# A final norm on VectorE alone, five weight buffers, and other queues for rows and form sources in a Strassen-form MLP

## The chip, the core and the metric

The kernel runs on one core of a Trainium2 chip. A core has five engines with instruction streams of their own: TensorE (PE in the profile, PEld for its weight loads), VectorE (DVE), ScalarE (ACT), GpSimd (POOL) and SyncE (SP). ACT, POOL and SP can each issue DMA transfers, in the order of their own streams. The metric is the device time of one execution in microseconds, as a median of several runs.

## The reference, cut to what matters

One layer of an encoder, in float32, on two batches with the same weights: `x_prompt` (512 tokens) and `x_sample` (1024 tokens), 1024 features each.

```
h = rms_norm(x, g_mix);  proj = h @ w_in                 # q, k, v, z, gates
merged = sigmoid(ga) * (attention @ w_branch_a) + sigmoid(gb) * (spatial gating @ w_branch_b)
x = x + merged @ w_out
h2 = rms_norm(x, g_mlp)
x = x + square(relu(h2 @ w_up)) @ w_down                 # w_up 1024 x 4096, w_down 4096 x 1024
y = rms_norm(x, g_final)
```

The change concerns the last three lines.

## The kernel before

**Products.** Every matrix product is made of float32r matmuls. A float32 operand is split into `hi` (a cast on ACT, L150) and `lo` (source minus hi, a subtraction on DVE, L151), and a product takes three matmuls (hi*hi, hi*lo, lo*hi). `weight` (L153 on) brings a weight block of 128 x 512: SP loads it into a buffer `raw` (L156, a ring of `N_RAW` = 3), ACT casts it and DVE subtracts, into a ring of five hi/lo pairs.

**Before the MLP.** Norm, projections, attention, gating and w_out run until about 1752 us. The last loop (L748 on) goes over the twelve token tiles t of 128 tokens: it adds `merged @ w_out` to x, stores the sum to `x1_scr` on SP's queue (L776), scales it by its root mean square (L782), transposes the halves on PE (L741), multiplies by `g_mlp` on DVE into `h2T` (L743, a ring of two buffers) and stores that to `h2_scr` on SP's queue (L746). The transposes of a tile come after the first matmuls of the next, so those of tile 11 come last of all.

**The MLP.** It takes the 1536 tokens as two groups g of 768 (tiles 0 to 5 and 6 to 11) and the 4096 hidden features as eight chunks c. Each product of a chunk is done by a form of Strassen's method with seven products, called p1, q6, q7, p2, q5, q4, q3, in place of eight. The sums of weight blocks that it needs were made during attention and lie in DRAM (`up_q`, `down_q`); those of activations are made on DVE. A chunk has two calls of `up_products` (j = 0, 1; together "an up stage": 2 x 7 forms of 12 matmuls of 128x384) and one of `down_products` (a "down stage": 126 matmuls of 128x512).

In an up stage each form's PSUM result is combined at once: p1 is copied by ACT (L888), then DVE makes v, z and the four blocks a11, a22, a21, a12 (L891 to L911), ACT applies relu and square (L870, L871), and `Forms.put`, `sums` and `last` build and split the seven forms of the activation (`act`; L817 to L819 and L828 on DVE, casts and subtractions in L150 and L151). In a down stage the results are added into rows `x` on DVE (L942 to L958) and, for a part, on POOL (L949, L950, L960).

Small tiles of 128x384 (`unit`, L797) come from one ring of twelve: p1, v, z, a, s, the form sources `h`, the differences `diff` and `raw_form`.

**Order.** Nothing sets times by hand but a list of side steps: `side()` is called after each form of an up stage and after each tile of a down stage, and runs the next step of the list. Engines run their own streams in order, and a DMA issue that waits for a buffer holds up what stands behind it in its queue.

- At the start of the MLP (L1062 to L1072), for each of four k: SP loads four form sources `h` from `h2_scr` (L1067), and ACT and DVE make the seven forms `hf` from them.
- `load_rows` (L1049) loads the group's six tiles of x, 512 KB each, from `x1_scr` on POOL's queue (L1052). It is called after c = 0's up stage; for g = 0 nothing holds the loads back but their buffers.
- For group 1 the sums of h are made in side steps of chunks 1 to 4 (`diff_steps`, loads and stores on SP's queue), and its `hf` forms in side steps of chunk 7 (`form_steps`, loads at L1013 on SP's queue).
- The final norm of group 0 runs as side steps in group 1's first up stage (`final_steps` with `spread`): squares on ACT, the root on DVE, then for each of twelve half tiles a scaling on ACT (L1038), a multiplication by g_final on POOL (L1039) and a store on POOL's queue (L1040). The rows of group 1 then take the same buffers.
- The final norm of group 1 comes at the end, as one DVE operation for each half tile (`normed`, L234).

Of the kernel before, what the change touches and what calls it, by code (L numbers as in the profile page):

```python
# [10 lines left out]
F32 = mybir.dt.float32  # L11
# [21 lines left out]
BIG = 1e30  # L33
ROW = 2 * 64 + 4
EDGE = 24
N_SPLIT, N_RAW = 5, 3
QT = 2
STEPS = 49 / 36
XSTEP = 4
# [67 lines left out]
def encoder_kernel(ctx: ExitStack, tc: tile.TileContext, a):  # L107
# [24 lines left out]
    v_scr = dram.tile([NTOK, NG * 512], F32, name="v_scr")  # L132
    gate_scr = [dram.tile([P, NTOK], F32, name=f"gate_scr{m}") for m in range(EARLY)]
    form_scr = dram.tile([len(DIFFS), 4, P, HT], F32, name="form_scr")
    h2_scr = dram.tile([KB, P, NTOK], F32, name="h2_scr")
    x1_scr = dram.tile([NTOK, DM], F32, name="x1_scr")
    up_sums = {k: dram.tile([DM // 2, DFF // 2], F32, name=f"up_{k}") for k in SUMS}
    down_sums = {k: dram.tile([DFF // 2, DM // 2], F32, name=f"down_{k}") for k in SUMS}
# [10 lines left out]
    def split(hi, lo, src, eng=nc.vector):  # L149
        nc.scalar.copy(hi, src)  # L150
        eng.tensor_sub(lo, src, hi.bitcast(F32))  # L151

    def weight(src, k, pair=None, eng=nc.vector):  # L153

        raw = wp.tile([P, 512], F32, tag="raw", name="raw", bufs=N_RAW).rearrange("p (k n) -> p k n", k=k)
        nc.sync.dma_start(out=raw, in_=src.rearrange("(k p) n -> p k n", p=P))  # L156
        if pair is None:
            pair = (wp.tile([P, 512], F32R, tag=s, name=s, bufs=N_SPLIT) for s in ("hi", "lo"))
        hi, lo = (t.rearrange("p (k n) -> p k n", k=k) for t in pair)
        split(hi, lo, raw, eng)  # L160
        return hi, lo
# [574 lines left out]
    def h_features(t, halves):  # L736

        for i, h in enumerate(halves):
            pt = tp_tile()
            for b in range(4):  # L740
                nc.tensor.transpose(pt[:, b * P:(b + 1) * P], h[:, b * P:(b + 1) * P], ident)  # L741
            hT2 = pp.tile([P, 512], F32, tag="half", name="h2T", bufs=2)
            nc.vector.tensor_mul(  # L743
                hT2.rearrange("p (k t) -> p k t", k=4), pt.rearrange("p (k t) -> p k t", k=4),
                g_mlp[:, 4 * i:4 * i + 4, None].to_broadcast([P, 4, P]))
            nc.sync.dma_start(  # L746
                out=h2_scr[4 * i:4 * i + 4, :, t * P:(t + 1) * P].rearrange("k p t -> p k t"),
                in_=hT2.rearrange("p (k t) -> p k t", k=4))  # L748

    for ch in range(2):  # L750
# [45 lines left out]
    slabs = ctx.enter_context(tc.tile_pool(name="slabs", bufs=6, side="right", reuse_waits="tile"))  # L796
    ps3 = ctx.enter_context(tc.tile_pool(name="ps3", bufs=8, space=PSUM, reuse_waits="tile"))  # L797
    def unit(name):
        return mp.tile([P, HT], F32, tag="unit", name=name, bufs=12)

    def bank():
        return ps3.tile([P, 512], F32, tag="acc", name="acc")
# [47 lines left out]
            self(len(self.steps))  # L850

    side = Side()

    def slab_view(s):
        return s.rearrange("p a b c -> p (a b c)").bitcast(F32)[:, :DM]
# [8 lines left out]
    def up_products(hf, j, forms, between):  # L864

        c = slice(j * P, (j + 1) * P)
        held = {}

        def squared(x, src):
            nc.scalar.activation(x, src, AF.Relu)  # L870
            nc.scalar.activation(x, x, AF.Square)  # L871

        for form in UP_ORDER:
            w = weight(block_of(a["w_up"][0], up_sums, form, DM // 2, DFF // 2, slice(0, DM // 2), c), 4)
            on = {"p2": "p1", "q3": "q5"}.get(form)
            acc = held[on] if on else bank()
            held[form] = acc
            acc = acc[:, :HT]
            for k in range(4):
                sh, sl = (x[:, k, :] for x in w)  # L880
                mh, ml = hf[k].of(form)
                for n, (st, mv) in enumerate(((sh, mh), (sh, ml), (sl, mh))):
                    nc.tensor.matmul(  # L883
                        acc, st, mv, start=not on and k == 0 and n == 0, stop=k == 3 and n == 2,
                        skip_group_check=bool(on))
            if form == "p1":
                p1 = unit("p1")
                nc.scalar.copy(p1, acc)  # L888
            elif form == "q6":
                v = unit("v")  # L890
                nc.vector.tensor_sub(v, acc, p1)  # L891
            elif form == "p2":
                a11 = unit("a11")
                squared(a11, acc)
                forms.put("p1", a11)
            elif form == "q7":
                z = unit("z")
                nc.vector.tensor_sub(z, v, acc)
            elif form == "q5":
                a22 = unit("a22")  # L900
                nc.vector.tensor_add(a22, z, acc)
                squared(a22, a22)
                forms.put("q4", a22)
            elif form == "q4":
                a21 = unit("a21")
                nc.vector.tensor_sub(a21, acc, z)
                squared(a21, a21)
                s2 = forms.sums(a11, a21, a22)
            elif form == "q3":
                a12 = unit("a12")  # L910
                nc.vector.tensor_add(a12, v, acc)  # L911
                squared(a12, a12)
                forms.last(a12, s2)
            between(form)
# [50 lines left out]
    def diff_steps(k):  # L965

        x = {}

        def load(key, r, s):
            x[key] = unit("diff")  # L970
            nc.sync.dma_start(out=x[key], in_=h2_scr[4 * s + k, :, GT + r * HT:GT + (r + 1) * HT])

        def store(form, key):
            nc.sync.dma_start(out=form_scr[DIFFS.index(form), k], in_=x[key])

        def first():
            load("a", 0, 0)
            load("b", 1, 0)
            nc.vector.tensor_sub(x["a"], x["a"], x["b"])
            store("q7", "a")  # L980

        def second():
            load("c", 1, 1)
            nc.vector.tensor_sub(x["b"], x["b"], x["c"])
            store("q5", "b")

        def third():
            nc.vector.tensor_add(x["c"], x["a"], x["c"])
            store("q6", "c")

        def fourth():
            load("d", 0, 1)
            nc.vector.tensor_sub(x["d"], x["d"], x["c"])
            store("q3", "d")

        return [first, second, third, fourth]

    def form_source(form, k):
        if form in DIFFS:
            return form_scr[DIFFS.index(form), k]  # L1000
        r, s = {"p1": (0, 0), "p2": (0, 1), "q4": (1, 1)}[form]
        return h2_scr[4 * s + k, :, GT + r * HT:GT + (r + 1) * HT]

    def form_steps(fs):

# [13 lines left out]
    def final_steps(g, x, tiles, g_final, spread):  # L1019
# [12 lines left out]
        def rows(j, i):  # L1032
# [2 lines left out]
            y = y_rows[6 * g + tiles[j]][:, i * 512:(i + 1) * 512]  # L1035
            gf = g_final[i]
            if spread:
                nc.scalar.activation(r, r, AF.Copy, scale=scale)  # L1038
                nc.gpsimd.tensor_mul(r, r, gf)  # L1039
                nc.gpsimd.dma_start(out=y, in_=r)  # L1040
            else:
                normed(r, r, scale, gf)
                (nc.scalar, nc.sync)[i].dma_start(out=y, in_=r)
# [4 lines left out]
    def load_rows(g):  # L1048
        x = {}  # L1049
        for t in (3, 4, 5, 0, 1, 2):  # L1050
            x[t] = mp.tile([P, DM], F32, tag="x", name="x", bufs=6)
            nc.gpsimd.dma_start(out=x[t], in_=x1_scr[(6 * g + t) * P:(6 * g + t + 1) * P, :])  # L1052
        return x

    def gains():
# [2 lines left out]
            load_g(g_final[i], a["g_final"][i * 512:(i + 1) * 512])  # L1058
        return g_final


    hf = {k: Forms("hf") for k in (3, 0, 1, 2)}  # L1062
    for k in range(4):
        parts = {}
        for s, r in ((0, 0), (0, 1), (1, 1), (1, 0)):
            parts[r, s] = unit(f"h{r}{s}")
            nc.sync.dma_start(out=parts[r, s], in_=h2_scr[4 * s + k, :, r * HT:(r + 1) * HT])  # L1067
        hf[k].put("p1", parts[0, 0])
        s2 = hf[k].sums(parts[0, 0], parts[1, 0], parts[1, 1])
        hf[k].put("q4", parts[1, 1])  # L1070
# [58 lines left out]
```

## Time and profile before

| | |
|---|---|
| median of 3 runs | 2783.99 us (2783.96 to 2785.03) |
| the profiled execution's own time | 2783.46 us |
| its span in the trace | 2781.7 us |
| mean granted TensorE clock | 0.987 |
| first up stage of group 0, from PE's first matmul | 1771.31 us |
| first down stage of group 0 | 1815.62 us |
| up and down stage of chunk 7, group 0 | 2198.44 and 2228.55 us |
| up stage of chunk 0, group 1 | 2266.46 us |
| its down stage | 2325.81 us |
| last down stage | 2734.63 us |

A row of the timeline has the start, the time that it spans, the engine, the line, the operation, output<-input, the shape and the count; in brackets the idle time of the engine before it and what ended that. "SPq" is an issue of a DMA. In the rows of waits stand the engine and tile that waited, what it waited for, the sum, the number and the longest. Names are those of the program without numbers; `h_scr` is `h2_scr`, `x_scr` is `x1_scr`, `s` are the sums s1 to s4, `p` is p1 in an up stage, `z` and `v` likewise.

### The profile page before, as it was taken

The page shows a single profiled execution, that of the slowest core. Times are in us where ns is not written, and L with a number is a line of the kernel's source. Part 1 is how long each engine was busy: PE and PEld are TensorE (multiplying, and loading weights), DVE is VectorE, ACT ScalarE, POOL GpSimd, SP SyncE. Part 2 cuts the span into 40 slices and gives each one's busy share as a digit, 9 for nine tenths or more (in the row PEclk, how much of TensorE's full clock was granted, in tenths as well). Part 3 has the DMA queues.
Part 4 walks back from the last instruction along what each step waited for, and adds up shares of the span by engine and source line. Part 5 has one row for each costly group of instructions (what it writes and reads, how often), then busy time and mean ns, then how long its engine had stood idle before and what let it go on. Part 6 is the DMA issues. An engine that isn't in the chain of part 4 may idle for free.

```text
span 2781.7 us, 38699 instructions
## 1 busy us (share of the span) xinstructions
PE 2681.2 (96%) x13400; PEld 2297.2 (83%) x13400; DVE 1731.4 (62%) x3665; ACT 1296.4 (47%) x2778; POOL 392.3 (14%) x418
## 2 busy tenths in 40 slices
PE   7999999999999999999999999699999978999997
PEld 5788888888888887888888888588889967998896
DVE  6542200166666666555555436688888887888887
ACT  5321111255566556553534321455555564665555
POOL 2000000011021212100000000022322134111321
PEclk9999999999999999999999999899999998999999
DMA  3112222237576767554444435545454455444443
GB/s 132 51 52 72 89 76 80 87 109 177 156 171 184 169 180 177 143 157 147 128 147 119 126 136 170 165 135 160 152 151 129 140 164 179 125 132 125 125 128 128
DMA packets 374516, 373.57 MB, mean 134 GB/s; under 512 B 21936, under 2 KB 294832, under 8 KB 370736
## 3 DMA queue, kind: packets, MB, share of 16 engines
q1 hardware_dynamic: 343344, 262.51, 31.4%
q0 software_dynamic: 21584, 66.90, 10.4%
q10 hardware_dynamic: 9392, 41.69, 4.5%
q8 instruction: 106, 1.74, 0.3%
q14 instruction: 90, 0.74, 0.1%
HBM read 321.95 MB, written 116.16 MB: 158 GB/s over the span
## 4 chain that ended last, share of the span: by engine, by line
PE 37%; DVE 8%; issue 5%; ACT 4%; DMA 3%; POOL 2%; SPq 0%; DVEq 0%; ACTq 0%; POOLq 0%
PE acc L933 9%; PE acc L175 7%; PE acc L176 7%; PE acc L177 7%; PE acc L883 6%; DVE lo L151 3%; DMA raw<-up_q 1%; ACT hi L150 1%; POOL x L950 1%; POOL x L949 1%; DVE act L151 1%; ACT a L870 1%; ACT a L871 1%; ACT act L150 1%; DVE x L958 1%
## 5 line engine op out<-in xcount | busy, mean ns | idle before, releaser
L151 DVE TENSOR_TENSOR lo<-raw,hi 128x512 fp32r<-128x512 f32 x694 | 545.1, 791 | 406.3 <-ACT hi L150 400.2
L150 ACT CAST hi<-raw 128x512 fp32r<-128x512 f32 x696 | 430.6, 620 | 647.0 <-PE acc L176 230.3
L175 PE MATMUL acc<-res_h,hi 128*128 128x512 f32 x1344 | 556.5, 414 | 0.8 <-DVE stg L576 0.8
L177 PE MATMUL acc<-res_h,lo 128*128 128x512 f32 x1344 | 526.8, 392 | 0.0
L176 PE MATMUL acc<-res_l,hi 128*128 128x512 f32 x1344 | 525.5, 391 | 0.0
L883 PE MATMUL acc<-hf,hi 128*128 128x384 f32 x1792 | 468.2, 342 | 42.0 <-ACT hf L150 16.8
L933 PE MATMUL acc<-hi,act 128*128 128x512 f32 x1344 | 420.2, 392 | 1.6 <-ACT hi L150 1.6
L883 PEld LDWEIGHTS acc<-hf,hi 128*128 128x128 f32 x1792 | 327.8, 191 | 56.7 <-ACT hf L150 20.6
L883 PE MATMUL acc<-hf,lo 128*128 128x384 f32 x896 | 303.4, 339 | 3.7 <-DVE lo L151 3.6
L933 PEld LDWEIGHTS acc<-hi,act 128*128 128x128 f32 x1344 | 254.3, 189 | 54.5 <-ACT hi L150 2.0
L177 PEld LDWEIGHTS acc<-res_h,lo 128*128 128x128 f32 x1344 | 252.6, 188 | 54.9
L175 PEld LDWEIGHTS acc<-res_h,hi 128*128 128x128 f32 x1344 | 254.1, 189 | 36.6 <-DVE stg L576 0.9
L176 PEld LDWEIGHTS acc<-res_l,hi 128*128 128x128 f32 x1344 | 254.5, 189 | 36.0
L933 PE MATMUL acc<-lo,act 128*128 128x512 f32 x672 | 264.7, 394 | 7.3 <-DVE lo L151 7.3
L548 ACT ACTIVATE pr<-pr,stg 128x128 f32<-128x128 f32 (+2 forms) x288 | 125.9, 438 | 177.1 <-DVE stg L545 140.7
L883 PEld LDWEIGHTS acc<-hf,lo 128*128 128x128 f32 x896 | 171.0, 191 | 5.2 <-DVE lo L151 5.2
L949 POOL TENSOR_TENSOR x<-x,z 128x512 f32<-128x512 f32 x48 | 71.2, 1484 | 623.0 <-DVE z L948 623.0
L933 PEld LDWEIGHTS acc<-lo,act 128*128 128x128 f32 x672 | 127.2, 189 | 37.0 <-DVE lo L151 10.7
L518 DVE TENSOR_TENSOR q<-qT,q 64x256 fp32r<-64x256 f32 x288 | 120.6, 419 | 48.0 <-ACT q L515 44.3
L560 DVE COPY pT<-tp 128x512 f32<-128x512 f32 (+1 forms) x144 | 82.1, 570 | 94.7 <-PE tp L558 93.7
L570 PEld LDWEIGHTS o<-v,pT 128*128 128x128 f32 x896 | 120.3, 191 | 25.0 <-DVE pT L560 14.7
L570 PE MATMUL o<-v,pT 128*128 128x64 f32 x896 | 117.3, 268 | 7.9 <-DVE pT L560 7.7
(183 smaller groups left out, 4081.8 us busy)
## 6 DMA issues: line engine op xcount, KB each, us to landing
raw<-in_w_in_dram SPq DMA_DIRECT2D x192, 256.0 KB, 3.1
raw<-up_q SPq DMA_DIRECT2D x128, 256.0 KB, 2.8
raw<-down_q SPq DMA_DIRECT2D x128, 256.0 KB, 2.7
raw<-in_w_up_dram SPq DMA_DIRECT2D x96, 256.0 KB, 2.8
raw<-in_w_down_dram SPq DMA_DIRECT2D x96, 256.0 KB, 2.8
up_q<-in_w_up_dram POOLq DMA_DIRECT2D x32, 512.0 KB, 9.2
down_q<-in_w_down_dram POOLq DMA_DIRECT2D x32, 512.0 KB, 10.4
raw<-in_w_branch_b_dram SPq DMA_DIRECT2D x48, 256.0 KB, 2.9
```

Source lines behind the costliest of these rows:

```text
L150: nc.scalar.copy(hi, src)
L151: eng.tensor_sub(lo, src, hi.bitcast(F32))
L175: nc.tensor.matmul(out, sh, mh, start=i == 0, stop=False)
L176: nc.tensor.matmul(out, sh, ml, start=False, stop=False)
L177: nc.tensor.matmul(out, sl, mh, start=False, stop=i == n - 1)
L518: nc.vector.tensor_sub(q2[rows, h, 1, :], src, q2[own, h, 0, :].bitcast(F32))
L548: last_of["act"] = nc.scalar.activation(pr[:, h, at:at + kn], pr[:, h, at:at + kn], AF.Exp, bias=low, scale=-1.0, accum_out=stg[:, j, 130 ...
L560: nc.vector.tensor_copy(self.pT[:, :n], pt[:, :n])
L570: nc.tensor.matmul(o[:, (2 * j + h) * 64:(2 * j + h + 1) * 64], self.pT[:, q * P:(q + 1) * P], found["v"][:, slot, h * 64:(h + 1) * 64], s ...
L883: nc.tensor.matmul(acc, st, mv, start=not on and k == 0 and n == 0, stop=k == 3 and n == 2, skip_group_check=bool(on))
L933: nc.tensor.matmul(acc, st, mv, start=not on and k == 0 and n == 0, stop=k == 1 and n == 2, skip_group_check=bool(on))
L949: nc.gpsimd.tensor_sub(x21, x21, z)
```

## The change

The norm of group 0 (`spread`) becomes one `normed` on DVE for each half tile; the stores stay on POOL's queue. In the MLP the raw ring grows from three to five buffers (two of them in the MLP's pool), and the ring of units shrinks from twelve to ten. `h2_scr` becomes one DRAM tensor for each group. The sixteen form sources of group 0 are loaded on POOL's queue instead of SP's, and the four `hf` slabs are taken in the order 0, 1, 2, 3. The rows of x for group 0 are loaded on ACT's queue instead of POOL's, and the loads for both groups may be issued only after the last p1 copy of chunk 0's up stage. All else, up to the MLP and at the program's end, is as it was.

```diff
-N_SPLIT, N_RAW = 5, 3
+N_SPLIT, N_RAW, MORE_RAW = 5, 3, 2
...
-    h2_scr = dram.tile([KB, P, NTOK], F32, name="h2_scr")
+    h2_scr = [dram.tile([KB, P, GT], F32, name=f"h2_scr{g}") for g in range(2)]
...
+    more_raw = []
+    def raw_tile():
+        pool, bufs = wp, N_RAW
+        if more_raw:
+            at = more_raw[1] = (more_raw[1] + 1) % (N_RAW + MORE_RAW)
+            if at >= N_RAW:
+                pool, bufs = more_raw[0], MORE_RAW
+        return pool.tile([P, 512], F32, tag="raw", name="raw", bufs=bufs)
...
     def unit(name):
-        return mp.tile([P, HT], F32, tag="unit", name=name, bufs=12)
+        return mp.tile([P, HT], F32, tag="unit", name=name, bufs=10)
...
     side = Side()
+    more_raw += [mp, 0]
...
             if form == "p1":
                 p1 = unit("p1")
-                nc.scalar.copy(p1, acc)
+                last_of["up"] = nc.scalar.copy(p1, acc)
...
             if spread:
-                nc.scalar.activation(r, r, AF.Copy, scale=scale)
-                nc.gpsimd.tensor_mul(r, r, gf)
+                normed(r, r, scale, gf)
                 nc.gpsimd.dma_start(out=y, in_=r)
...
         for t in (3, 4, 5, 0, 1, 2):
             x[t] = mp.tile([P, DM], F32, tag="x", name="x", bufs=6)
-            nc.gpsimd.dma_start(out=x[t], in_=x1_scr[(6 * g + t) * P:(6 * g + t + 1) * P, :])
+            eng = nc.gpsimd
+            if not g:
+                eng = nc.scalar
+            with tc.issue_after(last_of["up"].ins):
+                eng.dma_start(out=x[t], in_=x1_scr[(6 * g + t) * P:(6 * g + t + 1) * P, :])
...
-    hf = {k: Forms("hf") for k in (3, 0, 1, 2)}
+    hf = {k: Forms("hf") for k in range(4)}
     for k in range(4):
...
             parts[r, s] = unit(f"h{r}{s}")
-            nc.sync.dma_start(out=parts[r, s], in_=h2_scr[4 * s + k, :, r * HT:(r + 1) * HT])
+            nc.gpsimd.dma_start(out=parts[r, s], in_=h2_scr[0][4 * s + k, :, r * HT:(r + 1) * HT])
```

The rows of an engine's order below carry the line numbers of the changed kernel where they show it: from `weight` on its lines stand 11 higher, after `side` by 12 (L888 is L900, L911 is L923), L1040 is L1051, L1052 is L1067 and L1067 is L1081.

More of the change, by code (lines that the diff above doesn't have):

```diff
@@ L151, in split @@
         eng.tensor_sub(lo, src, hi.bitcast(F32))
+    more_raw = []
[6 more added lines that the diff above has]
+        return pool.tile([P, 512], F32, tag="raw", name="raw", bufs=bufs)
     def weight(src, k, pair=None, eng=nc.vector):
-        raw = wp.tile([P, 512], F32, tag="raw", name="raw", bufs=N_RAW).rearrange("p (k n) -> p k n", k=k)
+        raw = raw_tile().rearrange("p (k n) -> p k n", k=k)
         nc.sync.dma_start(out=raw, in_=src.rearrange("(k p) n -> p k n", p=P))
@@ L746, in h_features @@
             nc.sync.dma_start(
-                out=h2_scr[4 * i:4 * i + 4, :, t * P:(t + 1) * P].rearrange("k p t -> p k t"),
+                out=h2_scr[t // 6][4 * i:4 * i + 4, :, t % 6 * P:(t % 6 + 1) * P].rearrange("k p t -> p k t"),
                 in_=hT2.rearrange("p (k t) -> p k t", k=4))
@@ L970, in load @@
             x[key] = unit("diff")
-            nc.sync.dma_start(out=x[key], in_=h2_scr[4 * s + k, :, GT + r * HT:GT + (r + 1) * HT])
+            nc.sync.dma_start(out=x[key], in_=h2_scr[1][4 * s + k, :, r * HT:(r + 1) * HT])
         def store(form, key):
@@ L1001, in form_source @@
         r, s = {"p1": (0, 0), "p2": (0, 1), "q4": (1, 1)}[form]
-        return h2_scr[4 * s + k, :, GT + r * HT:GT + (r + 1) * HT]
+        return h2_scr[1][4 * s + k, :, r * HT:(r + 1) * HT]
     def form_steps(fs):
```

## The prediction

> **What bounds the kernel now.** I read the page's engine shares and its slices first, then windows of busy time, then the waits and the timeline where the windows dip.
>
> ```profile
> PE 2681.2 (96%) x13400; PEld 2297.2 (83%) x13400; DVE 1731.4 (62%) x3665; ACT 1296.4 (47%) x2778; POOL 392.3 (14%) x418
> ...
> PE   7999999999999999999999999699999978999997
> ```
>
> TensorE (PE) is the limit nearly everywhere: only slices 26, 33 and 34 dip inside the program. Windows give these dips (start and end, sum, then PE, PEld, DVE, ACT and POOL busy, the granted clock, DMA share, GB/s):
>
> ```profile
> 1750.00:1800.00 50.00, 28.89 (x111) 22.12 (x110) 33.11 (x78) 18.13 (x40) 2.63 (x5) 0.73 0.57 181
> 1800.00:1850.00 50.00, 49.68 (x248) 44.38 (x247) 42.86 (x71) 28.24 (x56) 13.39 (x9) 1.00 0.42 126
> 2228.00:2266.00 38.00, 30.73 (x116) 23.00 (x115) 35.14 (x58) 22.74 (x49) 10.04 (x8) 0.91 0.60 187
> 2266.00:2290.00 24.00, 21.93 (x111) 19.11 (x111) 17.99 (x37) 18.89 (x47) 9.12 (x8) 1.00 0.41 122
> 2290.00:2310.00 20.00, 7.91 (x30) 7.40 (x31) 20.00 (x13) 9.34 (x19) 19.60 (x24) 0.66 0.65 211
> 2310.00:2326.00 16.00, 9.56 (x45) 9.27 (x44) 7.30 (x14) 7.44 (x15) 1.10 (x3) 0.74 0.79 264
> 2326.00:2355.00 29.00, 29.00 (x126) 23.89 (x125) 23.01 (x36) 12.03 (x23) 8.90 (x6) 0.97 0.36 109
> 2355.00:2385.00 30.00, 29.27 (x168) 28.83 (x167) 24.77 (x41) 20.17 (x40) 4.68 (x3) 1.00 0.47 138
> ```
>
> The last two rows are a down stage of the MLP, 126 matmuls in 29.0 us, and an ordinary up stage, 168 in about 29.5. The first row is the **boundary** where the MLP begins. Rows three to six are the **switch** from token group 0 to group 1: chunk 7's down stage (2228 to 2266) and group 1's first up stage (2266 to 2326). That up stage takes 60 us for the work of 29.5. VectorE (DVE) is busy for all 20 us from 2290, GpSimd (POOL) for 19.6, and PE for 7.9. PE's waits over the switch (total, times, longest) say for whom:
>
> ```profile
> PE acc L883 <- ACT hi L150: 10.7, 3, 10.1
> PE acc L933 <- DVE lo L151: 6.8, 4, 3.0
> PE acc L883 <- DVE a L901: 6.4, 1, 6.4
> PE acc L883 <- DVE lo L151: 3.6, 3, 3.1
> ```
>
> **The boundary.** From its timeline:
>
> ```profile
> 1757.20 1.34 PE L741 MATMUL tp<-ident,h 128*128 128x128 f32 x8 [3.50 <-DVE h L782]
> 1765.00 1.33 DVE L743 TENSOR_TENSOR h2T<-tp,g_mlp 128x512 f32<-128x512 f32 x2 [7.55 <-DMA h_scr<-h2T]
> 1770.75 0.51 ACT L150 CAST hf<-h 128x384 fp32r<-128x384 f32 x1 [16.38 <-DMA h<-h_scr]
> 1752.82 2.67 POOL L1052 DMA_DIRECT2D x<-x_scr  x5 [32.29 <-DVE h L782]
> 1767.12 16.25 SPq L1067 DMA_DIRECT2D h<-h_scr  x16
> 1782.47 0.56 DVE L151 TENSOR_TENSOR hf<-s,hf 128x384 fp32r<-128x384 f32 x1 [0.58 <-ACT hf L150]
> 1788.29 0.56 DVE L151 TENSOR_TENSOR hf<-s,hf 128x384 fp32r<-128x384 f32 x1 [0.58 <-ACT hf L150]
> ```
>
> The last transposes end at 1758.54, yet their multiply starts at 1765.00: its buffer's store is still under way, behind five x loads of 512 KB (the fourth row). Then come the form sources on SP, and the first cast at 1770.75. From there DVE sets the pace: 5.82 us for each k of the forms (the last two rows).
>
> On POOL, before:
>
> ```order
> L467 DMA o_scr_83<-stg 64x4x132 x4
> L728 DMA g_mlp<-in_g_mlp_dram 128x8x1
> L1052 DMA x<-x_scr 128x1024 x6
> L949 TENSOR_TENSOR x<-x,z 128x512
> L950 TENSOR_TENSOR x<-x,z 128x512
> ```
>
> and now:
>
> ```order
> L478 DMA o_scr_83<-stg 64x4x132 x4
> L739 DMA g_mlp<-in_g_mlp_dram 128x8x1
> L1081 DMA h_15122<-h_scr_96 128x384
> L1081 DMA h_15124<-h_scr_96 128x384
> L1081 DMA h_15126<-h_scr_96 128x384
> ```
>
> The x rows' place is taken by sixteen form sources. Their scratch half holds tiles 0 to 5, stored long before, so they no longer wait for the last stores. But the first of them lands in memory that g_mlp held, so by the built program's waits it goes out only once the last h2T multiply has run: they do not move up into w_out. Without the x loads the multiply can start at 1758.6 and end at 1759.9; the first load then issues there instead of at 1767.12, 7.2 us earlier, and the first cast with it. Two things take back part. The first cast's tile lies over h2T buffers, so it needs the last h2T stores landed too, about when the first h load lands. And three weights that DVE split earlier now stand among the first forms, at 0.69 us each, with raws that SP fetches only then. I take **-4 us**, between -7 (all of it) and -1 (the split weights' loads arrive last).
>
> In this row of SP's queue a raw lands as usual in under 3 us, and in the next POOL's 256 KB stores in 2.4:
>
> ```profile
> raw<-up_q SPq DMA_DIRECT2D x128, 256.0 KB, 2.8
> ...
> sgu_scr<-u POOLq DMA_DIRECT2D x24, 256.0 KB, 2.4
> ```
>
> So I price the change of queue at nothing. The Trainium skill ("DMA: Bandwidth & Descriptors", Latency and other measured facts) gives the GpSimd path a first byte about 0.4 us later than SP's; by that the sum would be 0.4 us higher. The rows show no such difference, though they compare a store with a load.
>
> **The x rows of group 0** now go out on ACT's queue after chunk 0's second p1 copy:
>
> ```order
> L900 COPY p_15437<-acc 128x384
> L1067 DMA x<-x_scr 128x1024 x2
> L882 ACTIVATE a_15499<-acc 128x384
> L1067 DMA x<-x_scr 128x1024
> L883 ACTIVATE a_15499<-a_15499 128x384
> ```
>
> ACT issued no DMA here before; it now pays six issues, at POOL's 2.67/5 = 0.53 us some 3 us, in a window where it works 28.24 of 50. Their 3 MB join 126 GB/s (second window) where 264 GB/s were carried at 2310 to 2326. The rows are needed when the down stage begins, some 12 us (six forms) after that copy. A raw that is delayed is covered by five buffers at 2.1 us a form. I take **+1**, from 0 to +3.
>
> **Five raws, ten units.** In chunk 7's down stage PE takes 38 us for the 126 matmuls that take 29.0 in the next one: 9 lost, with 6.8 us of waits on lo. More raws let ACT and DVE start sooner, but DVE is busy 35.14 of 38, so little more than the idle 2.9 can go: **-2**, from 0 to -5 (work brought forward into the up stage, which has some DVE idle). In ordinary stages PE hardly waits (this row covers 1815 to 2228):
>
> ```profile
> PE acc L883 <- ACT p L888: 3.9, 6, 0.7
> ```
>
> A ring of ten units makes the second p1 copy reuse v's buffer, free after the L911 subtraction:
>
> ```profile
> 2216.07 0.55 DVE L911 TENSOR_TENSOR a<-v,acc 128x384 f32<-128x384 f32 x1
> 2218.98 0.47 ACT L888 COPY p<-acc 128x384 f32<-128x384 f32 x1
> ```
>
> There are 2.4 us to spare, so the other thirty stages get **0**, from -2 (raw jitter gone) to +3 (0.1 us a stage).
>
> **The norm at the switch.** What leaves, and what DVE suffers meanwhile:
>
> ```profile
> L1039 POOL TENSOR_TENSOR x<-x,g_final x12: 1266/1278/1304, 2285.2 to 2307.2; 128x512 f32<-128x512 f32 x12
> 2291.65 5.34 DVE L151 TENSOR_TENSOR act<-s,act 128x384 fp32r<-128x384 f32 x3
> 2299.73 9.28 DVE L151 TENSOR_TENSOR lo<-raw,hi 128x512 fp32r<-128x512 f32 x3
> 2326.79 1.50 DVE L151 TENSOR_TENSOR act<-s,act 128x384 fp32r<-128x384 f32 x3
> 2320.53 0.69 DVE L151 TENSOR_TENSOR lo<-raw,hi 128x512 fp32r<-128x512 f32 x1 [1.10 <-ACT hi L150]
> 2765.54 4.06 DVE L234 SCALAR_TENSOR_TENSOR x<-x,rs_y,g_final 128x512 f32<-128x512 f32 x6
> ```
>
> Beside POOL's multiplies three act subtractions take 5.34 us and three lo's 9.28; alone 1.50 and about 2.05. That is 11.1 us of stretch, which goes with the multiplies. What comes is the operation of the last row: 12 x 4.06/6 = 8.1 us on DVE. ACT loses 12 scalings. So DVE's demand from 2266 to 2326 falls from 17.99 + 20.00 + 7.30 = 45.3 to 45.3 - 11.1 + 8.1 = 42.3 us: still far above the 29.5 of PE, and the stage cannot be hidden. What counts is which of DVE's work PE waits for. DVE before, where the second half's weights begin:
>
> ```order
> L151 TENSOR_TENSOR act<-s_20539,act 128x384
> L151 TENSOR_TENSOR lo<-raw,hi 128x512 x3
> L891 TENSOR_TENSOR v<-acc,p_20571 128x384
> L151 TENSOR_TENSOR lo<-raw,hi 128x512 x2
> L898 TENSOR_TENSOR z<-v,acc 128x384
> ```
>
> and now:
>
> ```order
> L151 TENSOR_TENSOR act<-s_20537,act 128x384
> L245 SCALAR_TENSOR_TENSOR x<-x,rs_y,g_final 128x512
> L903 TENSOR_TENSOR v<-acc,p_20567 128x384
> L245 SCALAR_TENSOR_TENSOR x<-x,rs_y,g_final 128x512 x2
> L151 TENSOR_TENSOR lo<-raw,hi 128x512
> L245 SCALAR_TENSOR_TENSOR x<-x,rs_y,g_final 128x512 x2
> L151 TENSOR_TENSOR lo<-raw,hi 128x512
> ```
>
> Seven norms stand ahead of these rows and five among them, so the lo of the second half's third form (q7) waits for nine of the twelve. DVE's subtraction of the first half's q4 is the anchor:
>
> ```profile
> 2284.71 0.55 DVE L906 TENSOR_TENSOR a<-acc,z 128x384 f32<-128x384 f32 x1
> 2288.01 1.09 DVE L817 TENSOR_TENSOR s<-a,a 128x384 f32<-128x384 f32 x1 [0.90 <-ACT a L871]
> ```
>
> It came at 2284.71, and with raws less late I put it at 2281. From it to that lo DVE has 3.3 us until the first s (the gelu on ACT), then 3 s, 1 a, 1 s4, 1 v and 5 act at about 0.5 (5.5), seven norms at 0.68 (4.8; two fit into the 3.3) and the lo (0.7): 14.3 us, so about 2295.4. PE will stand there, some 8 us. Then five forms at 2.1 us are left, 10.4, and some 2 us for a clock that is low after a stall (0.66 from 2290): the stage ends near 2308 instead of 2325.8, -18. I take **-17**. Ends: -24 if the lo does not bind, and -8 if each of the nine norms costs a further us of alternation with ACT.
>
> POOL keeps the stores, and each waits for its norm on DVE:
>
> ```order
> L1051 DMA out_y_prompt_dram<-x 128x512 x2
> L1067 DMA x<-x_scr 128x1024
> L1051 DMA out_y_sample_dram<-x 128x512 x4
> L1067 DMA x<-x_scr 128x1024
> L1051 DMA out_y_prompt_dram<-x 128x512 x6
> L1067 DMA x<-x_scr 128x1024 x4
> ```
>
> Queued behind them stand the last four x loads of group 1, which go out after the last norm, at about 2299; before, the last went out at 2315.85:
>
> ```profile
> 2315.85 0.53 POOL L1052 DMA_DIRECT2D x<-x_scr  x1 [5.28 <-DMA out_y_prompt_dram<-x]
> ```
>
> and PE's next down stage then lost nothing to speak of, so I add nothing.
>
> **Sum.** -4 + 1 - 2 + 0 - 17 = -22 us on the profiled execution's 2783.46 us (span 2781.7, 1.8 us around it), so 2761.5; the median of the runs, 2783.99, is 0.5 higher: **2762**. The ends add up to -38 (2746) and -3 (2781).
>
> **Rivals.**
> 1. *DVE at the switch gives back half.* Norms, acts and gelus alternate between DVE and ACT, and the switch gains 8 instead of 17: 2771. For it: the demand of 42.3 us above. Against: before's worst stretch was POOL's. Chance 0.17.
> 2. *The best ends together*: 2746 to 2754; the lo's do not bind and DVE catches up in the down stage, where it worked 23.01 of 29 us (2326 to 2355). Chance 0.11.
>
> 3. *POOL's issues are held up by DVE.* Sixteen loads now pass GpSimd while DVE works without pause. Were each held as the lo's were beside POOL, (9.28 - 2.05)/3 = 2.4 us, twelve would need 29 us against the 17.5 of three k's, +11: 2773. Against: five loads went out in 2.67 us from 1752.82, with DVE at work:
>
> ```profile
> 1753.47 1.28 DVE L743 TENSOR_TENSOR h2T<-tp,g_mlp 128x512 f32<-128x512 f32 x2
> ```
>
>    The Trainium skill ("SBUF — State Buffer", SBUF: two separate sides) speaks against this change in that way: DVE operations in a two-port mode keep GpSimd from writing descriptors. Under Who interferes with whom it excepts tensor_tensor, the only kind among the forms' steps. Chance 0.04.
> 4. *Nothing changes* (same): what leaves at the switch is taken by the norms ahead of the lo's and the boundary waits as before for the last h2T stores: within 5 us. The demand on DVE falls by only 3 us, which speaks for it. Chance 0.05.
> 5. *Slower.* SP's queue is in order; with ten units the difference loads of chunks 1 to 4 and the form loads of chunk 7 wait longer for a unit, and raws behind them starve PE. Such a starved weight is known here: 5.41 us for ACT, 6.4 for PE.
>
> ```profile
> 2315.96 0.62 ACT L150 CAST hi<-raw 128x512 fp32r<-128x512 f32 x1 [5.41 <-DMA raw<-in_w_up_dram]
> ```
>
> It decides once a unit comes free over 10 us (five raws) late; one such stall in each of the five chunks is +32: 2794. Against: the 2.4 us to spare. Chance 0.07.
>
> **Numbers.** The forecast's own case (2755 to 2769) has 0.56. The range 2747 to 2776 leaves out rivals 4 and 5 and some of 2, some 0.17. A run of this kernel can tell about 0.2% (5.6 us) from no change: faster is the forecast with rivals 1 to 3, 0.88; same 0.05; slower 0.07.
>
> **What would show it.** Right: the multiply at the boundary follows its transposes without a wait on DMA; first cast near 1763; act subtractions at 0.5 us each at the switch; PE waits once, for a lo, some 8 us around 2290 (less the boundary's gain); that up stage about 42 us. Wrong: a wait of POOL or DVE for h at each k; up stages of other chunks over 30.5 us; PE waiting for x in chunk 0's down stage; a switch as long as before.

## The result

| | median us | runs |
|---|---|---|
| before | 2783.97 | 2780.84 to 2785.03 (4) |
| changed | 2762.88 | 2758.58 to 2765.74 (4) |

The ratio is 0.9925, 95% interval 0.9908 to 0.9942: 21 us faster, where 22 had been forecast. The profiled execution of the changed kernel took 2758.58 us, the quickest of its four, 24.9 less than that of before. So the places below add up to 24.9, not to 21.

The page shows the same PE work in a shorter span. The three dips in the slices are each one step shallower (slice 26 from 6 to 7, 33 from 7 to 8, 34 from 8 to 9):

```profile
PE 2679.2 (97%) x13400; PEld 2295.7 (83%) x13400; DVE 1722.9 (62%) x3677; ACT 1289.0 (47%) x2766; POOL 382.6 (14%) x416
...
PE   7999999999999999999999999799999989999997
```

By stage, from the first matmul of each stage in PE's timeline (us; group 1's chunk 0 before is taken from 2266.00, its first matmul, not from the 2266.46 given among the times before):

| place | before | after | change | forecast |
|---|---|---|---|---|
| start of the first up stage, and that stage | 1771.31, 44.31 | 1765.87, 45.58 | -4.2 | -4 |
| first down stage | 28.60 | 32.24 | +3.6 | +1 |
| chunk 7's down stage | 37.45 | 34.95 | -2.5 | -2 |
| up stage of group 1's chunk 0 | 59.81 | 45.13 | -14.7 | -17 |
| all the rest | | | -7.2 | 0 |

**The boundary** goes by the mechanism forecast, with a smaller gain at its start. Timeline of the changed kernel, DVE, ACT and POOL (L754 is the h2T multiply, L1081 the form sources):

```profile
1759.63 0.69 DVE L754 TENSOR_TENSOR h2T<-tp,g_mlp 128x512 f32<-128x512 f32 x1 [0.16 <-PE tp L752]
1765.31 0.51 ACT L150 CAST hf<-h 128x384 fp32r<-128x384 f32 x1 [10.48 <-DMA h<-h_scr]
1760.89 3.35 POOL L1081 DMA_DIRECT2D h<-h_scr  x6 [140.94 <-DVE h2T L754]
```

The multiply follows its transposes; no DMA stands before it. The loads follow the multiply, and the first cast comes 5.4 us earlier than the 1770.75 of before (7.2 had been forecast at most). The stage itself, with three weights among its first forms, is 1.3 us longer.

**The first down stage** lost what the forecast had not seen. PE, then ACT and its DMA issues (ACTq):

```profile
1816.54 0.49 PE L945 MATMUL acc<-hi,act 128*128 128x512 f32 x1 [2.84 <-ACT hi L150]
```

```profile
1803.22 0.61 ACT L150 CAST hi<-raw 128x512 fp32r<-128x512 f32 x1
1803.95 0.34 ACTq L1067 DMA_DIRECT2D x<-x_scr  x1
...
1804.56 0.47 ACT L900 COPY p<-acc 128x384 f32<-128x384 f32 x1
...
1814.14 0.33 ACTq L1067 DMA_DIRECT2D x<-x_scr  x1
...
1815.87 2.70 ACT L150 CAST hi<-raw 128x512 fp32r<-128x512 f32 x5
```

From the cast at 1803.2 to 1815.9 ACT casts no further weight, though SP had fetched them (its last issue of a raw before that ends at 1804.9, the next comes only at 1817.2); then it casts five in a row, and PE has waited.

**The switch.** PE's two longest waits in the up stage of group 1's chunk 0, and on DVE the anchor of the forecast (L918, was L906) and the lo that PE waits for:

```profile
2286.53 0.62 PE L895 MATMUL acc<-hf,hi 128*128 128x384 f32 x2 [1.45 <-ACT p L900]
2290.94 0.69 PE L895 MATMUL acc<-hf,lo 128*128 128x384 f32 x1 [3.79 <-DVE lo L151]
```

```profile
2277.89 0.55 DVE L918 TENSOR_TENSOR a<-acc,z 128x384 f32<-128x384 f32 x1
2281.82 1.02 DVE L151 TENSOR_TENSOR act<-s,act 128x384 fp32r<-128x384 f32 x2
2290.21 0.68 DVE L151 TENSOR_TENSOR lo<-raw,hi 128x512 fp32r<-128x512 f32 x1
```

Act subtractions take half a microsecond each again. From the anchor to the end of that lo pass 13.0 us (forecast 14.3), and from there the stage takes 12.4 more, as forecast. But the anchor comes 19.7 us after the stage's first matmul (2258.21), where before had 18.7 and the forecast 15: those 4.7 us, less the 1.3, make the stage 45.1 us long instead of the forecast's 42. PE, late itself, stands at that lo for 3.8 us and not for 8. The windows (same columns as before) show where the stage still loses: PE is busy for 1.75 of 7 us while DVE is busy for all 7, and the clock is at 0.76 afterwards:

```profile
2223.00:2258.00 35.00, 29.40 (x114) 21.65 (x113) 33.43 (x55) 23.04 (x49) 10.03 (x8) 0.95 0.64 203
2284.00:2291.00 7.00, 1.75 (x10) 1.11 (x8) 7.00 (x13) 2.82 (x6) 3.28 (x7) 0.93 0.74 225
2291.00:2303.30 12.30, 12.02 (x52) 11.70 (x53) 8.28 (x14) 4.14 (x8) 4.95 (x10) 0.76 0.98 359
```

**A correction on the change.** The loads of group 1 were said to wait for the p1 copy. On POOL's queue they do not:

```profile
2283.63 0.54 POOL L1067 DMA_DIRECT2D x<-x_scr  x1 [2.28 <-issue]
```

```profile
2286.00 0.47 ACT L900 COPY p<-acc 128x384 f32<-128x384 f32 x1
```

`issue_after` sets the place in the program's order. In the stream of the copy's own engine (ACT, group 0) that keeps the load behind what stands ahead of it, but doesn't make it wait for the copy's end: the first row went out at 1803.95, the copy ran at 1804.56 (rows above). On another engine's queue it makes no wait.

### The profile page after: what moved, and what is told of

Its sections match the earlier page's. It is cut to its first block, busy times and chain, and to the rows that moved or that the text cites. A ratio compares the mean times of both kernels' runs of the same rounds, so it can differ in the third digit from the quotient of the medians.

```text
span 2756.8 us, 38688 instructions
## 1 busy us (share of the span) xinstructions
PE 2679.2 (97%) x13400; PEld 2295.7 (83%) x13400; DVE 1722.9 (62%) x3677; ACT 1289.0 (47%) x2766; POOL 382.6 (14%) x416
## 3 DMA queue, kind: packets, MB, share of 16 engines
q1 hardware_dynamic: 341040, 259.36, 31.4%
## 4 chain that ended last, share of the span: by engine, by line
PE 51%; DVE 4%; ACT 2%; DMA 2%; issue 1%; POOL 0%; SPq 0%; DVEq 0%; ACTq 0%
PE acc L895 15%; PE acc L945 14%; PE acc L186 7%; PE acc L188 7%; PE acc L187 7%; DVE lo L151 1%; DVE hf L151 1%; DVE x L245 0%; ACT hi L150 0%; PE tp L752 0%; DVE act L151 0%; PE o L581 0%; DMA diff<-h_scr 0%; PE s L542 0%; ACT a L882 0%
## 5 line engine op out<-in xcount | busy, mean ns | idle before, releaser
L151 DVE TENSOR_TENSOR lo<-raw,hi 128x512 fp32r<-128x512 f32 x694 | 537.7, 781 | 392.9 <-ACT hi L150 388.8
L895 PE MATMUL acc<-hf,hi 128*128 128x384 f32 x1792 | 465.7, 341 | 14.4 <-ACT hf L150 10.8
L945 PE MATMUL acc<-hi,act 128*128 128x512 f32 x1344 | 419.1, 391 | 5.2 <-ACT hi L150 4.6
L895 PEld LDWEIGHTS acc<-hf,hi 128*128 128x128 f32 x1792 | 328.1, 191 | 26.5 <-ACT hf L150 14.3
L895 PE MATMUL acc<-hf,lo 128*128 128x384 f32 x896 | 302.8, 339 | 5.7 <-DVE lo L151 5.7
L945 PEld LDWEIGHTS acc<-hi,act 128*128 128x128 f32 x1344 | 253.0, 188 | 59.0 <-ACT hi L150 5.9
L945 PE MATMUL acc<-lo,act 128*128 128x512 f32 x672 | 264.1, 393 | 5.9 <-DVE lo L151 5.7
L895 PEld LDWEIGHTS acc<-hf,lo 128*128 128x128 f32 x896 | 171.0, 191 | 7.4 <-DVE lo L151 7.4
L945 PEld LDWEIGHTS acc<-lo,act 128*128 128x128 f32 x672 | 126.6, 188 | 36.4 <-DVE lo L151 10.4
L529 DVE TENSOR_TENSOR q<-qT,q 64x256 fp32r<-64x256 f32 x288 | 120.7, 419 | 48.0 <-ACT q L526 44.3
## 6 DMA issues: line engine op xcount, KB each, us to landing
down_q<-in_w_down_dram POOLq DMA_DIRECT2D x32, 512.0 KB, 10.1
```

The lines of the kernel that those rows point to most:

```text
L529: nc.vector.tensor_sub(q2[rows, h, 1, :], src, q2[own, h, 0, :].bitcast(F32))
L895: nc.tensor.matmul(acc, st, mv, start=not on and k == 0 and n == 0, stop=k == 3 and n == 2, skip_group_check=bool(on))
L945: nc.tensor.matmul(acc, st, mv, start=not on and k == 0 and n == 0, stop=k == 1 and n == 2, skip_group_check=bool(on))
```

## The experiments

Two theories: **T**, each part acts at its own place, and the switch's gain is the norm's; **R**, the five weight buffers carry PE over the switch, and the norm matters little. Ratios are against the kernel before on the same chip, with 95% intervals.

**1. The norm alone.**

```diff
 # before.py
-                nc.scalar.activation(r, r, AF.Copy, scale=scale)
-                nc.gpsimd.tensor_mul(r, r, gf)
+                normed(r, r, scale, gf)
```

> The kernel before with the norm of group 0 on VectorE and nothing else of the change. Theory T (each part acts at its own place: the norm at the switch, the weight buffers in the ordinary stages and chunk 7, the loads at the boundary): group 1's first up stage falls from 59.8 us by 11 to 15, all else stays, so 2769 to 2773 us. Rival R (at the switch it is the five weight buffers that carry PE over, and the norm only moves work of equal length from GpSimd's stretch to VectorE): that stage falls by under 5 us, so 2779 or more.

Measured: 2775.36 us, 0.9966 (0.9953 to 0.9979), -9 us: a gain between those of T and R. The up stage fell from 59.8 to 44.3 us, more than T asked, but the down stage after it rose from 29.6 to 34.7. In that down stage (L933) PE now waits for a lo:

```profile
2320.06 0.79 PE L933 MATMUL acc<-lo,act 128*128 128x512 f32 x1 [2.79 <-DVE lo L151]
```

With three raws the backlog is only handed on: part of the gain is given back a stage later.

**2. The change without its norm, and the raws alone.**

```diff
 # no_norm: after.py
-                normed(r, r, scale, gf)
+                nc.scalar.activation(r, r, AF.Copy, scale=scale)
+                nc.gpsimd.tensor_mul(r, r, gf)
```

> The changed kernel with the norm of group 0 as before (scaling on ScalarE, multiplication on GpSimd). T: the switch goes back by 11 to 15 us, so 2774 to 2778 us. R: under 4 us is lost, so 2767 or less.

Measured: 2767.15 us, 0.9940 (0.9923 to 0.9956). That is what R expected.

```diff
 # raws_only: before.py with raw_tile() of the change, and
-        return mp.tile([P, HT], F32, tag="unit", name=name, bufs=12)
+        return mp.tile([P, HT], F32, tag="unit", name=name, bufs=10)
```

> The kernel before with five raw buffers and ten units and nothing else. T: chunk 7's down stage falls by some 2.5 us, the ordinary up stages by 0.7 each (the wait for the p1 copy goes), the switch by under 4: 2772 to 2776 us. R: the switch's up stage falls by 10 or more besides, so 2766 or less. If the p1 waits stay at 0.6 a stage, five raws aren't what took them away in the changed kernel.

Measured: 2767.27 us, 0.9939 (0.9924 to 0.9954), -17 us: between the two, near R. The switch (from chunk 7's down stage to group 1's second up stage) takes 115.2 us, 126.8 before and 108.7 in the changed kernel. The up stages of chunks 1 to 7 take 29.4 to 29.8 us each instead of 29.9 to 31.4. ACT's waits from 1845 to 2222, first before, then with five raws, say why:

```profile
ACT hi L150 <- DMA raw<-in_w_up_dram: 35.1, 23, 2.4
ACT hi L150 <- PE acc L933: 32.5, 20, 3.6
ACT hi L150 <- DMA raw<-up_q: 28.6, 28, 1.7
ACT hi L150 <- DMA raw<-in_w_down_dram: 22.7, 20, 3.4
ACT hi L150 <- DMA raw<-down_q: 10.6, 5, 2.5
ACT hi L150 <- PE acc L883: 9.3, 8, 1.3
```

```profile
ACT hi L150 <- PE acc L945: 84.6, 34, 3.4
ACT hi L150 <- PE acc L895: 45.1, 32, 1.8
```

With three raws the cast waits mostly for its load to land (97 us, against 42 for PE); with five it waits for PE to give back a hi buffer. ACT, in order, was late with everything behind such a cast, the p1 copies too: PE's 3.9 us of waits for p in these chunks, shown in the prediction, are gone with five raws.

And since no_norm and raws_only agree within 0.1 us, the loads' part is worth nothing with rows on ACT's queue: the boundary's gain is lost again in the first down stage.

**3. The multiplies of GpSimd by themselves.** The kernel of no_norm without them, so that group 0's output lacks the multiplication by g_final:

```diff
 # no_gain: after.py
-                normed(r, r, scale, gf)
+                nc.scalar.activation(r, r, AF.Copy, scale=scale)
```

> The changed kernel with the norm of group 0 as a scaling on ScalarE alone: the multiplication by g_final is left out of group 0's output. VectorE's order is that of the run no_norm, so the two differ by GpSimd's twelve multiplies alone. Theory (beside them VectorE's subtractions are stretched, and only that makes no_norm 4 us slower than the changed kernel): three act subtractions take 1.5 instead of 5.4 us, the up stage is 9 to 12 us shorter than no_norm's 51.5, and the time is 2754 to 2759 us, below the changed kernel, which pays 8 us of norms on VectorE. Rival (the twelve scalings on ScalarE, ahead of its casts, cost the time): within 3 us of no_norm, 2764 to 2768.

Measured: 2757.42 us, 0.9914 (0.9899 to 0.9928): 9.7 us below no_norm by the medians, 7 by the ratios (0.9940, whose interval overlaps a little). The up stage falls from 51.5 to 41.6 us, the whole switch from 115.0 to 108.5, for the down stages on both sides of it are longer (the profiled execution, 2761.76 us, is 4 us above the other three). DVE at the switch, no_norm, then no_gain:

```profile
2285.20 5.41 DVE L151 TENSOR_TENSOR act<-s,act 128x384 fp32r<-128x384 f32 x3
...
2291.00 1.96 DVE L151 TENSOR_TENSOR act<-a,act 128x384 fp32r<-128x384 f32 x1
...
2298.35 3.48 DVE L151 TENSOR_TENSOR lo<-raw,hi 128x512 fp32r<-128x512 f32 x1 [2.35 <-ACT hi L150]
```

```profile
2289.68 1.49 DVE L151 TENSOR_TENSOR act<-s,act 128x384 fp32r<-128x384 f32 x3
...
2292.72 0.56 DVE L151 TENSOR_TENSOR act<-a,act 128x384 fp32r<-128x384 f32 x1 [0.46 <-ACT act L150]
...
2298.49 0.69 DVE L151 TENSOR_TENSOR lo<-raw,hi 128x512 fp32r<-128x512 f32 x1 [3.26 <-ACT hi L150]
```

The same subtractions in the same order take 1.49 instead of 5.41 us, and the three pairs of rows differ by 8.1 us together. So the norm's account, with five raws: GpSimd's multiplies cost 7 to 10 us by the times and 6.5 at the switch. The changed kernel is 4 us below no_norm by the times and 6.3 at the switch (115.0 to 108.7). What twelve operations on DVE cost in their place, less ACT's scalings, is not clear of the noise: 3 to 5.5 us by the times (0.9925 less 0.9914 of 2784; 2762.88 - 2757.42), with intervals that overlap, and almost nothing by the switches (108.7 and 108.5).

The Trainium skill ("SBUF — State Buffer", Who interferes with whom) says that a VectorE instruction with two SBUF inputs contends with a GpSimd instruction that reads SBUF, and that the second blocks until the first is through. In size this pair agrees: one act of 0.56 us took 1.96 beside multiplies of 1.28, about the sum. Which of the two came first, the rows don't settle.

**4. The rows of x on another queue.**

```diff
 # rows_on_pool: after.py
-                eng = nc.scalar
+                eng = nc.gpsimd
```

> The changed kernel with group 0's x rows on GpSimd's queue instead of ScalarE's, issued after the same p1 copy. Theory: the first down stage lost 3.6 us because the row loads on ScalarE's queue put the casts of its weights behind them in ScalarE's order; with the loads on GpSimd two casts stand right after the p1 copy again, and the stage falls from 32.2 to about 28.6: 3 to 4 us faster than the changed kernel, about 2759. Rival: the rows' 3 MB delay the weights on the DMA engines whatever the queue: the stage stays above 31 us and the time within 1 us.

Measured: 2757.18 us, 0.9902 (0.9888 to 0.9917); the first down stage 28.61 us. The stage is as the theory said, but the run doesn't tell it from its rival: on POOL the rows were not held back at all (see the correction above), and went out between form sources:

```profile
1761.87 2.11 POOL L1067 DMA_DIRECT2D x<-x_scr  x4
```

So the next run forced the wait, by a copy that GpSimd can make only once the second half's form p1 is there:

```diff
 # rows_wait: rows_on_pool, load_rows(g, act)
+            if not g and t == 3:
+                nc.gpsimd.tensor_copy(x[t][:, :1], act[1].slab[:, 0, 0, :1].bitcast(F32))
```

> The changed kernel with group 0's x rows on GpSimd's queue behind a copy of one column that needs chunk 0's second activation form, so that they really go out in the second half of the first up stage; ScalarE issues none, and its order has casts of weights right behind the p1 copy. Theory (it was the row loads in ScalarE's stream that put the casts late): the first down stage takes 28.6 to 29.5 us, the first up stage starts as in the changed kernel, and the whole is 2757 to 2760 us. Rival (rows that late delay the weights on the DMA engines): the stage stays at 31 us or more, and the time within 1.5 us of the changed kernel's.

Measured: 2756.71 us, 0.9903 (0.9888 to 0.9919); the first down stage 28.60 us.

```profile
1811.01 3.15 POOL L1069 DMA_DIRECT2D x<-x_scr  x6 [0.30 <-issue]
```

All six rows go out within 3.2 us, the first four later than ACT had them, with the down stage starting at 1812.21, and PE waits for nothing in it. The rows' traffic is harmless; their place in ACT's stream was the cost. This run and rows_on_pool are the fastest measured, some 6 us below the changed kernel by medians and ratios (0.9903 and 0.9925, whose intervals overlap a little). Shown by the trace are the stage's 3.6 us; the profiled executions are 1.7 apart, as that of the changed kernel was its quickest.

**5. The boundary's two edits.**

```diff
 # rows_late: before.py
-            nc.gpsimd.dma_start(out=x[t], in_=x1_scr[...])
+            with tc.issue_after(last_of["up"].ins):
+                nc.gpsimd.dma_start(out=x[t], in_=x1_scr[...])
```

> The kernel before, but group 0's x rows are issued only after chunk 0's last p1 copy, on GpSimd's queue as before; form sources stay on SyncE. Theory A (the rows' 3 MB, not the form sources' queue, hold the boundary up: they delay the store that the last h2T multiply waits for): the multiply's wait of 7.55 us goes, PE's first matmul of the MLP comes 5 to 6 us earlier (near 1766), the first down stage starts 4 to 5 us earlier (near 1811) and the whole is 2779 to 2780 us, 4 to 5 below before. Rival B (the form sources' place behind the last stores in SyncE's queue sets it): the multiply comes earlier, but the first cast by under 2 us, and the time stays within 2 us of before.

Measured: 2783.71 us, 1.0003 (0.9994 to 1.0013). This run did not do what was meant: the rows went out as before, at 1754.76 (in a run whose MLP lies 1.9 us later), so it says nothing on A or B. It only confirms that `issue_after` makes no wait here.

```profile
1754.76 2.67 POOL L1054 DMA_DIRECT2D x<-x_scr  x5 [32.29 <-DVE h L782]
```

```diff
 # h_on_pool: before.py with h2_scr in two tensors, hf in the order 0, 1, 2, 3, and
-            nc.sync.dma_start(out=parts[r, s], in_=h2_scr[...])
+            nc.gpsimd.dma_start(out=parts[r, s], in_=h2_scr[0][...])
```

> The kernel before, with h2_scr in two tensors, the form sources of group 0 on GpSimd's queue and the hf slabs in the order 0, 1, 2, 3; the x rows stay on GpSimd's queue without the wait for the p1 copy, and stand behind the first four and the next four form sources there. A: the store of h2T no longer meets the rows, since they stand behind the first sources, so the multiply's wait goes here too and the first cast comes 5 us earlier; but four rows of 512 KB then stand ahead of the second k's sources, which come some 8 us later than they could, so at most 2 us are left: 2782 to 2785 us. B: the queue is what counts, so 4 us or more below before.

Measured: 2780.41 us, 0.9991 (0.9981 to 1.0000). The first cast comes 5.25 us earlier, as A said:

```profile
1765.50 0.51 ACT L150 CAST hf<-h 128x384 fp32r<-128x384 f32 x1 [10.31 <-DMA h<-h_scr]
...
1773.52 0.51 ACT L150 CAST hf<-h 128x384 fp32r<-128x384 f32 x1 [2.16 <-DMA h<-h_scr]
```

The second k's sources, behind four rows, cost 2.2 us (A had put it at 8 later than possible), and the first down stage starts 2.9 us earlier than before. The time, 2 to 3 us below before, falls between A's and B's. On one queue the sources push the rows behind them, so this run has the rows' move in it too. Which of the two frees the store can be read from units_10 (under 6 below), where the sources stay on SP and the rows go out 7.9 us earlier than before:

```profile
1744.97 2.67 POOL L1052 DMA_DIRECT2D x<-x_scr  x5 [31.13 <-DVE h L782]
```

```profile
1757.11 1.47 DVE L743 TENSOR_TENSOR h2T<-tp,g_mlp 128x512 f32<-128x512 f32 x2 [3.89 <-DMA h_scr<-h2T]
...
1763.01 0.69 DVE L743 TENSOR_TENSOR h2T<-tp,g_mlp 128x512 f32<-128x512 f32 x1 [0.16 <-PE tp L741]
```

There too the last multiply waits for no store; an earlier one does. So it is the rows that hold the store up, and the queue of the sources isn't needed to free it. From the end of the last multiply to the first cast it takes 4.4 and 4.0 us with the sources on SP (before, units_10), 5.0 and 4.8 on POOL (changed, h_on_pool): by itself that queue gains nothing.

**6. Order and depth.**

```diff
 # norms_spread: rows_on_pool, and
-                side.add([lambda: None] * 2 + final_steps(0, ...))
+                side.add(final_steps(0, ...))      # each of the twelve row steps followed by an empty step
```

> The changed kernel with group 0's x rows on GpSimd's queue (as in rows_on_pool), and the norms as side steps of every second call instead of every call, without the two empty steps ahead of the squares: on VectorE the lo of the second half's third form then waits for six norms instead of nine, and the later ones stand between lo's one by one. Theory (PE waits at the switch for the lo's behind the norms): PE's wait of 3.8 us for a lo falls to under 2, the up stage by 2 to 3, and the time is 2754 to 2756 us. Rival (VectorE's sum of work sets the stage, whatever its order): no change from rows_on_pool, 2757 +- 1.5.

Measured: 2758.65 us, 0.9918 (0.9901 to 0.9934), as the rival said. PE's waits at the switch, first in the changed kernel, then here:

```profile
PE acc L895 <- DVE lo L151: 4.7, 3, 3.8
PE acc L945 <- DVE lo L151: 4.6, 4, 2.5
```

```profile
PE acc L945 <- DVE lo L151: 7.1, 6, 2.5
PE acc L895 <- DVE lo L151: 2.1, 3, 1.1
```

What the up stage (L895) no longer waits for, the down stage (L945) waits for.

```diff
 # units_10: before.py
-        return mp.tile([P, HT], F32, tag="unit", name=name, bufs=12)
+        return mp.tile([P, HT], F32, tag="unit", name=name, bufs=10)
```

> The kernel before with ten units instead of twelve and nothing else. Theory: the ring has two buffers to spare, no stage moves by more than 0.2 us, and the time stays within 2 us of before. Rival: the loads of differences and forms wait for units, chunks 1 to 4 and 7 lose 1 us or more each, so 5 us or more.

Measured: 2780.36 us, 0.9990 (0.9981 to 1.0000). Not slower, as expected, and 2 to 3 us faster. In its profile the MLP begins 3.0 us earlier than in that of before, with the rows of x out of the store's way as shown under 5; that the smaller ring lets them out by moving the buffers in memory is argued, not shown. Of the stages of chunks 1 to 6 none moves by over 0.5 us (0.2 had been expected). The smaller ring costs nothing. The run raws_only has it too, and its MLP begins 1.7 us earlier than before, so its 17 us may not all be the raws'.

```diff
 # raws_4: raws_only, and
-N_SPLIT, N_RAW, MORE_RAW = 5, 3, 2
+N_SPLIT, N_RAW, MORE_RAW = 5, 3, 1
```

> The kernel before with four raws and ten units. VectorE's order at the switch has the second half's lo's behind the act subtractions, as before and unlike with five. Theory (raws act in two ways: a fourth covers the latency of the loads in ordinary stages, and a fifth lets two more lo's be done ahead of the stretch that GpSimd's multiplies cause at the switch): the ordinary up stages lose their p1 wait (29.45 us each) but the switch gains little: 2774 to 2778 us. Rival (only the supply of weights counts, wherever it is short): four give at least two thirds of what five gave, 2773 or less, with the switch 8 us or more shorter.

Measured: 2771.59 us, 0.9960 (0.9945 to 0.9974): two thirds of what five raws gave, the ordinary up stages at 29.45 us, and the switch 9.0 us shorter (117.8). The theory of two separate effects falls, for the fourth buffer already gives most at the switch, with the second half's lo's still behind the act subtractions. The fifth gives 4 to 6 us more. PE's longest wait at the switch is for a cast still:

```profile
PE acc L895 <- ACT hi L150: 12.4, 4, 9.1
```

```diff
 # three_raws: after.py
-    more_raw += [mp, 0]
-        return mp.tile([P, HT], F32, tag="unit", name=name, bufs=10)
+        return mp.tile([P, HT], F32, tag="unit", name=name, bufs=12)
```

> The changed kernel with three raws and twelve units, as before. If the parts add up (norm alone -9, loads about 0 with the rows on ScalarE's queue), 2774 to 2776 us; if the norm on VectorE is worth more without the deep buffers or the loads gain when ScalarE's casts are late anyway, 2772 or less; if three raws cannot stand the rows' late traffic in chunk 0, 2778 or more.

Measured: 2772.80 us, 0.9963 (0.9951 to 0.9976), -10 us: about the norm alone with loads worth nothing, between two of the cases. The raws are thus worth 10 us on top of the rest, and 17 by themselves.

## Why the prediction was right, and where it was not

The time was forecast to within 1 us, but partly because errors cancelled.

- **Boundary, -4: right** (-4.2), by the mechanism given: the store no longer behind the rows, the loads behind the last multiply, 7.2 us at most, part taken back by three weights. The cast gained 5.4 us of the 7.2, for the first load issued 1.0 us later than forecast and landed later; the stage gave back 1.3. One reading was off: the change of queue was priced at nothing, from a load and a store on different queues. The same 192 KB sources, before and after:

```profile
h<-h_scr SPq DMA_DIRECT2D x16, 192.0 KB, 3.2
```

```profile
h<-h_scr POOLq DMA_DIRECT2D x16, 192.0 KB, 4.0
```

They land 0.8 us later from POOL. Other traffic beside them differs too, but raws_only, with raws beside the sources and all on SP's queue, has 3.3 us; so the longer first byte that the Trainium skill gives for that path ("DMA: Bandwidth & Descriptors", Latency and other measured facts: 0.4 us) pointed the right way, and the measurement is larger still. Rival 3 did not come: with DVE at work two issues took 1.07 us (1767.40), no more each than the six in 3.35 us from 1760.89, with DVE idle.

```profile
1767.40 1.07 POOL L1081 DMA_DIRECT2D h<-h_scr  x2 [3.17 <-DVE s L828]
```

- **x rows, +1: wrong by 2.6** (+3.6, outside the 0 to +3 given). The step that failed is "in a window where it works 28.24 of 50": it counted ACT's issue time and not the order of its stream. The rows of ACT's order quoted there have no cast of weights behind the p1 copy, where the kernel before has two; the forecast read them for the loads alone. Before:

```profile
1807.36 0.47 ACT L888 COPY p<-acc 128x384 f32<-128x384 f32 x1
...
1809.35 1.24 ACT L150 CAST hi<-raw 128x512 fp32r<-128x512 f32 x2 [1.11 <-DMA raw<-in_w_up_dram]
```

rows_wait shows the order, not the traffic, to be the cause.
- **Five raws, -2 in chunk 7: right** (-2.5). **The other stages, 0: wrong by 7** (-7.2, below the -2 given). The step that failed is "in ordinary stages PE hardly waits": the row beside it already has 3.9 us, and the up stages of 29.9 to 31.4 us against 29.4 say that each lost half a microsecond or more. Those waits hang on casts that wait for loads.
- **Switch, -17: nearly the size (-14.7), but not for the reason given.** The forecast put it down to the norm, but for an anchor some 4 us earlier "with raws less late", and the anchor did not come earlier. Alone the norm gives 9 to 10 us over the whole, the raws alone 11.6 at the switch and 17 in all, and both together 18.1 at the switch. Taken out of the finished kernel the norm is worth 4 to 6 us, the raws 10. What the forecast had right is the norm's inner account: the stretch goes (6.5 to 10 us by no_gain), DVE pays for the norms (some 8 us of operations, and 5.5 at most of the time), DVE's sum of work still bounds the place (norms_spread), and one lo behind nine norms stops PE. What it lacked is that three raws held back the same lo's: PE's longest wait before was for a cast, 10.1 us, and the text took only the DVE side of it.
- **Slower, rival 5: no.** A ring of ten units costs nothing (units_10).

What stays open: why the changed kernel's runs spread over 7 us, what the norms on DVE cost within 0 to 5.5 us, and why the rows go out earlier with ten units.

## What to carry to other kernels

Where an engine's work is a chain load, cast, subtract, look at what ended the idle time of the first step in ordinary stages: casts that waited for loads meant too few arriving buffers here, both in ordinary stages and at the switch. A DMA issue put on a compute engine's queue can cost more than its issue time (six of 0.33 to 0.45 us cost a stage 3.6 us here): ask which instructions now stand behind it in that stream. And price each part of a change also as what it is worth with the others in place; parts that feed the same wait do not add up (9 and 17 gave 21).

## What the runs showed of the hardware

Twelve GpSimd multiplies of 1.28 us cost the program 6.5 to 10 us through VectorE (no_norm and no_gain), about half of their own 15 us or more, by stretching two-input subtractions beside them. Six row loads, 3 MB in all, issued from GpSimd's queue within 3.2 us at the start of a down stage (rows_wait; 351 GB/s from 1811 to 1822) cost that stage nothing visible: 28.60 us.
